# Hybrid block on one core: gate rows through device memory, the last mean square on VectorE, queries turned in the values' bank

## The chip, the core and the metric

One Trainium2 chip, of which one core is used. A core has TensorE (matrix products, written PE in the profile, with its weight loads as PEld), VectorE (DVE), ScalarE (ACT), GpSimd (POOL) and SyncE (SP), which issues most transfers, and 16 DMA engines. The engines run side by side, each its own instructions in order, and wait for each other through semaphores. TensorE writes to PSUM, which has eight banks of 512 fp32 columns on 128 partitions; everything else lies in SBUF, and the weights come from device memory. The metric is the time of one execution on the device in microseconds (us), as the median of several runs.

## The reference

One layer on 256 tokens of width 2048, in fp32: a normalised and modulated input is projected by `w_in`, goes through a two-way gated linear recurrence with 16 heads and through windowed attention with 16 query heads over 4 key heads, both results are projected and merged, and the merged sum is projected by `w_out`, scaled by a gate, added to the input and normalised. Cut to the lines that matter for the change:

```python
mod = jax.nn.silu(c) @ w_ada[l] + b_ada[l]
shift, scale, gate = jnp.split(mod[:, None, :], 3, axis=-1)
xn = rmsnorm(h, norm_gain[l]) * (1.0 + scale) + shift
aq, ak, av, ag, hq, hff, hfb, hi, hg, ma, mb = split_columns(xn @ w_in[l])
q = apply_axial_rope(aq.reshape(B, n, ATT_HEADS, ATT_HEAD_DIM), cos, sin) * q_scale
k = apply_axial_rope(ak.reshape(B, n, ATT_KV_HEADS, ATT_HEAD_DIM), cos, sin)
att_branch = window_attention(q, k, v, k_c, v_c, sink_logits[l]) * jax.nn.silu(ag)
...
y_a = hg_branch @ w_o_hgrn_l
y_b = att_branch @ w_o_attn_l
y = jax.nn.sigmoid(m_a + b_m[0]) * y_a + jax.nn.sigmoid(m_b + b_m[1]) * y_b
h = h + gate * (y @ w_out_l)
return rmsnorm(h, final_norm_gain)      # y * rsqrt(mean(y*y) + EPS) * gain
```

## The kernel before

**Weights.** Every fp32 product is made of three products with rounded operands (`mm3`, lines 80 to 83): a high part of each operand and a low rest. `wchunk` (lines 67 to 78) loads a chunk of 512 KB into one of four `raw` buffers, ScalarE rounds it to `wh` (line 74, three buffers) and VectorE takes the rest `wl` (line 75, three buffers). A rounding into a `wh` buffer waits until TensorE has used up the chunk that lay there. Projections accumulate in four PSUM banks (`pj`). The other four banks have one buffer each by tag: `tp` (turnings), `al1` and `al2` (scores and the recurrence's levels), `o` (state products, outputs of the recurrence, values).

**The gate.** `gates` (lines 750 to 758) forms the gate vector on VectorE beside the recurrence, in four pieces of 512 columns. `gate_end` (line 195) turns a piece with four TensorE transposes into the bank `tp` (`tqg`), and VectorE reduces it (`redg`, line 200) into `gcol`, which holds the gate with the channel on the partition, 128 x 16. Just behind the third piece stand the transposes `to` of a recurrence pair (line 696), in the same bank `tp`. Before the output projection the gate is needed as rows that are equal on all partitions: lines 1047 to 1055 make four diagonal matrices from `gcol` on VectorE (`dgm`), multiply each by a matrix of ones on TensorE in plain fp32 (`pg`, 128 x 512, two passes), and ScalarE copies them to `gt`.

**Attention.** A list written by hand sets TensorE's order here (`manual_schedule`, lines 865 to 1011); the scheduler orders ScalarE and VectorE around it, with attention's own work ahead. `alternate(attend(sts), fill(sts), 1)` takes one step of attention, then one weight chunk of filler. `attend` has two steps for each of 32 heads-by-block `n`: the scores (`sc`), and then, for every fourth, the values of the four before (`oba`, 12 products into the bank `o`), followed by the turning of the probabilities of `n - 2` (`tkp`, four transposes into `tp`). `values` ends with VectorE reading `oba` (`br`, line 980), which alone frees the bank `o`. `fill` runs groups 1 to 3 of `group_in`, while attention works on the group before: eight chunks of the query projection, then eight chunks (slots 0 to 7, two halves of four) of the attention gate's projection. Between these chunks the queries of the group are rotated (`rope`, VectorE) and turned: `turn_q(t)` for token blocks 0 and 1 makes four transposes `tkq` (line 914), a rounding on ScalarE (line 916) and the rest on VectorE (line 917, `qTa`). Block 0 is turned after slot 1 and block 1 after slot 3, in the bank `tp`. After the first half of the gate's chunks ScalarE and VectorE finish two heads: a copy and a sum (`hsum`), a sigmoid (`ga`, line 937) and a product (line 938). The sigmoid and the exponential of the scores (line 956) need different function tables on ScalarE, and each change is an ACT_TABLE_LOAD. The rotated queries, `hsum` and `br` share two buffers (tag `bb`).

**The end.** `settle` (line 1059) multiplies the output projection by `gt`, adds the input, and takes the sum of squares with ScalarE (line 1067). For the last 256 columns this is followed by a sum over five partial sums on VectorE (line 1096), a mean on GpSimd (line 178), a power -1/2 on GpSimd (line 179), the scaling and the stores.

Of the kernel before, what the change touches and what calls it, by code (L numbers as in the profile page):

```python
# [7 lines left out]
F32 = mybir.dt.float32  # L8
F32R = mybir.dt.float32r
U8 = mybir.dt.uint8  # L10
AF = mybir.ActivationFunctionType
ALU = mybir.AluOpType
PSUM = bass.MemoryType.PSUM

P = 128
# [22 lines left out]
def block_kernel(ctx: ExitStack, tc: tile.TileContext, x, c, cx, c_ctx, w_ada, b_ada, norm_gain, w_in,  # L38
# [4 lines left out]
    def pl(name, bufs=1, **kw):  # L43
        return tc.tile_pool(name=name, bufs=bufs, **kw)
# [6 lines left out]
    wp = ctx.enter_context(pl("wp"))  # L51
    pj = ctx.enter_context(pl("pj", 4, space=PSUM))
    ps = ctx.enter_context(pl("ps", 1, space=PSUM))

    def row_bcast(src, n):
        return bass.AP(src.tensor, src.offset, [[0, P], [1, n]])
# [136 lines left out]
                dve.scalar_tensor_tensor(acc, wr[:, j, :], cc, acc, op0=ALU.mult, op1=ALU.add)  # L193

    def gate_end(acc, g):
        tq = ps.tile([P, 512], F32, tag="tp", name="tqg")
        for q in range(4):
            pe.transpose(tq[:, q * P: (q + 1) * P], acc[:, q * P: (q + 1) * P], ident)
        red = pad.tile([P, 4], F32, tag="redg", name="redg")
        dve.tensor_reduce(red, tq.rearrange("p (q k) -> p q k", q=4), mybir.AxisListType.X, ALU.add)  # L200
        gv = gcol[:, 4 * g: 4 * g + 4]
        dve.tensor_tensor(gv, red, gv, op=ALU.add)
# [8 lines left out]

    cg = pad.tile([P, KT], F32, name="cg")
    gcol = few.tile([P, KT], F32, name="gcol")

    FIRST = (("F0", 2), ("F1", 1), ("F0", 2))
    with pl("st", reuse_waits="tile") as st:
# [533 lines left out]
    def gates():  # L750

        for g in range(4):
            for k0 in range(0, KT, 2):
                gate_chunk(accT[:, 0, :], g, k0)
                yield
            gate_end(accT[:, 0, :], g)
        while True:
            yield

# [105 lines left out]
    with tc.manual_schedule(engines={mybir.EngineType.PE}):  # L865
# [29 lines left out]
        def keys():  # L895
            for t in range(4):
# [5 lines left out]
                split(dst[0], dst[1], tk.rearrange("p (j t) -> p j t", j=4))  # L902
                yield

        def group_in(j, st):

            bq = yield from proj_tok_g(w_in, C_Q + 512 * j, x_st, range(2))
            def turn_q(t):
                qr = base.tile([P, 4, HD], F32, tag="bb", name="qr", bufs=2)
                rope(qr, bq[t], t)  # L910
                yield
                tk = ps.tile([P, 512], F32, tag="tp", name="tkq")
                for i in range(4):
                    pe.transpose(tk[:, i * P: (i + 1) * P], qr[:, i, :], ident)
                qh, ql = [X[:, t].rearrange("p h t -> p (h t)") for X in st["q"]]
                act.activation(qh, tk, AF.Copy, scale=HD ** -0.5)
                dve.scalar_tensor_tensor(ql, tk, HD ** -0.5, qh.bitcast(F32), op0=ALU.mult, op1=ALU.subtract)

            turning = [turn_q(t) for t in range(2)]
            next(turning[0])  # L920
            st["q"] = [at.tile([P, 2, 4, P], F32R, tag=tg, name="qTa") for tg in Q_TAGS[j % 2]]
            st["g"] = gt_tile(j, [P, 4, T], "ga")
            for hf in range(2):
                bg = proj_col_x_g(w_in, C_G + 512 * j + 256 * hf)
                for k0 in range(0, KT, 4):
                    next(bg)
                    yield
                    if (hf, k0) == (0, 4):
                        next(turning[0], None)
                    if (hf, k0) == (0, 0):  # L930
                        next(turning[1])
                    if (hf, k0) == (0, 12):
                        next(turning[1], None)
                for i, b in enumerate(result(bg)):
                    gs = halves_sum(b, "bb", 2)
                    gi = st["g"][:, 2 * hf + i, :]
                    act.activation(gi, gs, AF.Sigmoid)
                    dve.tensor_tensor(gi, gi, gs, op=ALU.mult)
# [78 lines left out]
    for t in range(2):  # L1017
        nc.sync.dma_start(xv[t], x[t * P: (t + 1) * P, :])
        nc.sync.dma_start(fg[t], row_bcast(fin_gain[t * 1024: (t + 1) * 1024], 1024))

    def part_b(n):
        by = proj_tok(w_oa, n * 512, b_st, range(2))
# [21 lines left out]
        sl = slice(t * P, (t + 1) * P)  # L1044
        return XH[:, kt, sl], XL[:, kt, sl]

    ones = base.tile([P, 512], F32, tag="sm", name="ones", bufs=3)[:, :P]
    pool.memset(ones, 1.0)
    for n in range(4):
        pg = ps.tile([P, 512], F32, tag="o", name="pg")  # L1050
        dg = base.tile([P, 4, P], F32, tag="bb", name="dgm", bufs=2)
        for q in range(4):
            dve.tensor_scalar(dg[:, q, :], ident, gcol[:, 4 * n + q: 4 * n + q + 1], None, op0=ALU.mult)
        pe.matmul(pg, ones, dg.rearrange("p q c -> p (q c)"), start=True, stop=True)
        act.activation(gt[n // 2][:, (n % 2) * 512: (n % 2 + 1) * 512], pg, AF.Copy)
    fin = few.tile([P, 14], F32, name="fin")
    ssf = fin[:, :10].rearrange("p (t n) -> p t n", t=2)
    rsf = fin[:, 10:12]
    def settle(t, bo, c0, width, slot, gain=True):

        cl = slice(c0, c0 + width)
        ch = slice(c0 % 1024, c0 % 1024 + width)
        ht = base.tile([P, 512], F32, tag="bb", name="ht", bufs=2)[:, :width]
        dve.tensor_tensor(ht, bo, gt[c0 // 1024][:, ch], op=ALU.mult)
        dve.tensor_tensor(xv[t][:, cl], xv[t][:, cl], ht, op=ALU.add)
        sq = base.tile([P, 512], F32, tag="sm", name="fsq", bufs=3)[:, :width]
        act.activation(sq, xv[t][:, cl], AF.Square, accum_out=ssf[:, t, slot: slot + 1])
        if gain:
            dve.tensor_tensor(xv[t][:, cl], xv[t][:, cl], fg[c0 // 1024][:, ch], op=ALU.mult)

# [16 lines left out]
            split(bH[:, ks, :], bL[:, ks, :], rv)  # L1087
    for t in range(2):
        settle(t, bo[t][:, :256], D - 512, 256, 3)
    for t in range(2):  # L1090
        be = bank()
        for kt in range(KT):
            mm3(be[:, :256], y_st(kt, t), (bH[:, kt, :], bL[:, kt, :]), kt == 0, kt == KT - 1)
        settle(t, be[:, :256], D - 256, 256, 4, False)
        tot = fin[:, 12 + t: 13 + t]
        dve.tensor_reduce(tot, ssf[:, t, :], mybir.AxisListType.X, ALU.add)
        rs = rsf[:, t: t + 1]
        rstd_of(tot, D, rs)
        for c0, c1, on_act in ((0, 512, True), (512, 1024, False), (1024, 1536, True), (1536, D, False)):
            o_ = xv[t][:, c0: c1]  # L1100
            if on_act:
                act.activation(o_, o_, AF.Copy, scale=rs)
            else:
                e = min(c1, D - 256)
                dve.tensor_scalar(xv[t][:, c0: e], xv[t][:, c0: e], rs, None, op0=ALU.mult)
                if e < c1:
                    dve.scalar_tensor_tensor(xv[t][:, e: c1], xv[t][:, e: c1], rs, fg[1][:, e - 1024: c1 - 1024],
                                             op0=ALU.mult, op1=ALU.mult)
            (nc.scalar if on_act else nc.sync).dma_start(out[t * P: (t + 1) * P, c0: c1], o_)
# [53 lines left out]
```

## Time and profile before

| | |
|---|---|
| median of 3 runs | 1657.49 us (1657.47 to 1657.75) |
| the profiled execution, whole | 1657.43 us |
| its span in the trace | 1655.7 us |
| TensorE busy | 1632.2 us of the span (99%) |
| VectorE, ScalarE, GpSimd busy | 969.2 us, 750.8 us, 34.5 us |
| DMA | 274.16 MB, mean 166 GB/s |

The span is what the trace covers; 1.7 us of the execution lie around it. A row of a timeline gives the start of an instruction (us from the start of the span), its duration, the engine, the line and what it writes and reads; in brackets stands how long the engine sat idle before it and whom it waited for. Matmuls overlap: the next of 512 columns starts 0.23 us after the one before, though each is shown with 0.39 us, so a loss on TensorE is read from the starts. The granted clock (PEclk) is 1.00 at 2.4 GHz and 0.50 at 1.2 GHz.

### The profile page before, as it was taken

How to read it: one execution, taken by the hardware profiler on the slowest of the kernel's cores; microseconds unless marked ns; L12 is line 12 of the kernel's file. 1: busy time of each engine (PE TensorE's matmuls, PEld its weight loads, DVE VectorE, ACT ScalarE, POOL GpSimd, SP SyncE). 2: the span in 40 equal slices, each digit the busy share in tenths (PEclk: the TensorE clock that was granted, in tenths of full speed). 3: DMA queues.
4: the chain of work that ended last, by engine and by line, in shares of the span. 5: the costliest groups of instructions: out<-in, count | busy, mean ns of one | idle time of the engine just before them, and what ended most of it. 6: DMA issues, size and time to landing. Idle time of an engine off the chain costs nothing.

```text
span 1655.7 us, 22835 instructions
## 1 busy us (share of the span) xinstructions
PE 1632.2 (99%) x8897; PEld 1345.2 (81%) x8897; DVE 969.2 (59%) x1511; ACT 750.8 (45%) x1143; POOL 34.5 (2%) x88
## 2 busy tenths in 40 slices
PE   7999999999999999999999999999999999999997
PEld 4558888888888888888888888888888888788887
DVE  4444577636765466754667555325677676555565
ACT  4333444324443344423455443223576787444443
POOL 2000000000000000000000000000000000000000
PEclk9999999999999999999999999999999999999999
DMA  9993444346344453435345666434544455665554
GB/s 357 382 382 113 147 138 148 102 127 191 91 127 127 149 175 98 139 102 168 125 117 159 185 195 196 129 102 137 171 139 152 132 165 156 207 205 190 179 180 138
DMA packets 191100, 274.16 MB, mean 166 GB/s; under 512 B 9728, under 2 KB 112400, under 8 KB 190224
## 3 DMA queue, kind: packets, MB, share of 16 engines
q1 hardware_dynamic: 189344, 269.39, 51.3%
q0 software_dynamic: 928, 2.20, 0.5%
q8 instruction: 70, 1.15, 0.3%
q10 hardware_dynamic: 720, 1.11, 0.2%
q14 instruction: 38, 0.31, 0.1%
HBM read 270.57 MB, written 2.10 MB: 165 GB/s over the span
## 4 chain that ended last, share of the span: by engine, by line
PE 97%; DVE 1%; DMA 1%; ACT 1%; issue 0%; POOLq 0%; POOL 0%; ACTq 0%
PE pj L81 23%; PE pj L82 23%; PE pj L83 23%; PE pj L139 7%; PE pj L144 3%; PE al L556 2%; PE pa L301 2%; PE pj L391 1%; PE tkp L970 1%; PE pj L384 1%; PE sb L633 1%; PE pj L385 1%; DMA raw<-in_w_ada_dram 1%; PE sc L83 0%; PE ob L674 0%; PE sc L81 0%
## 5 line engine op out<-in xcount | busy, mean ns | idle before, releaser
L75 DVE TENSOR_TENSOR wl<-raw,wh 128x1024 fp32r<-128x1024 f32 x392 | 479.1, 1223 | 430.9 <-ACT wh L74 430.6
L74 ACT ACTIVATE wh<-raw 128x1024 fp32r<-128x1024 f32 x392 | 414.7, 1058 | 576.7 <-PE pj L83 415.9
L83 PE MATMUL pj<-wh,xHL 128*128 128x512 f32 (+1 forms) x1024 | 396.8, 388 | 0.0
L82 PE MATMUL pj<-wl,xHL 128*128 128x512 f32 (+1 forms) x1024 | 395.7, 387 | 0.4 <-DVE wl L75 0.4
L81 PE MATMUL pj<-wh,xHL 128*128 128x512 f32 (+1 forms) x1024 | 392.2, 390 | 0.0
L83 PEld LDWEIGHTS pj<-wh,xHL 128*128 128x128 f32 x1024 | 192.4, 188 | 39.7 <-issue 0.7
L82 PEld LDWEIGHTS pj<-wl,xHL 128*128 128x128 f32 x1024 | 192.5, 188 | 38.5 <-DVE wl L75 0.7
L81 PEld LDWEIGHTS pj<-wh,xHL 128*128 128x128 f32 x1024 | 192.2, 188 | 38.8 <-issue 1.0
L139 PE MATMUL pj<-xHL,wh 128*128 128x512 f32 x512 | 180.9, 396 | 0.0
L81 PE MATMUL pj<-xHL,wh 128*128 128x512 f32 x416 | 164.4, 395 | 0.0
L83 PE MATMUL pj<-xHL,wl 128*128 128x512 f32 x416 | 162.2, 390 | 0.0
L82 PE MATMUL pj<-xHL,wh 128*128 128x512 f32 x416 | 162.1, 390 | 0.0
L144 PE MATMUL pj<-xHL,wl 128*128 128x256 f32 x512 | 139.3, 282 | 0.0
L139 PEld LDWEIGHTS pj<-xHL,wh 128*128 128x128 f32 x512 | 95.1, 188 | 19.5
L82 PE MATMUL pj<-wl,bH 128*128 128x512 f32 x256 | 100.0, 390 | 0.0
L83 PE MATMUL pj<-wh,bL 128*128 128x512 f32 x256 | 99.7, 389 | 0.0
L144 PEld LDWEIGHTS pj<-xHL,wl 128*128 128x128 f32 x512 | 96.6, 189 | 2.5
L83 PEld LDWEIGHTS pj<-xHL,wl 128*128 128x128 f32 x416 | 78.1, 188 | 16.4
L81 PEld LDWEIGHTS pj<-xHL,wh 128*128 128x128 f32 x416 | 78.2, 188 | 15.7
L82 PEld LDWEIGHTS pj<-xHL,wh 128*128 128x128 f32 x416 | 78.2, 188 | 15.5
L81 PE MATMUL pj<-wh,bH 128*128 128x512 f32 x256 | 89.9, 390 | 0.1
L599 DVE TENSOR_TENSOR A<-A,X 128x512 f32<-128x512 f32 x96 | 62.0, 687 | 15.9 <-ACT so L533 6.1
(272 smaller groups left out, 1749.7 us busy)
## 6 DMA issues: line engine op xcount, KB each, us to landing
raw<-in_w_in_dram SPq DMA_DIRECT2D x292, 512.0 KB, 3.6
raw<-in_w_ada_dram SPq DMA_DIRECT2D x128, 256.0 KB, 5.4
raw<-in_w_ada_dram SPq DMA_DIRECT2D x32, 512.0 KB, 3.8
raw<-in_w_o_hgrn_dram SPq DMA_DIRECT2D x32, 512.0 KB, 3.7
raw<-in_w_o_attn_dram SPq DMA_DIRECT2D x32, 512.0 KB, 3.8
raw<-in_w_out_dram SPq DMA_DIRECT2D x32, 512.0 KB, 4.4
raw<-in_w_in_dram SPq DMA_DIRECT2D x24, 256.0 KB, 5.5
X<-in_x_dram SPq DMA_DIRECT2D x2, 1024.0 KB, 6.3
```

The source lines that it names most:

```text
L74: act.activation(h[:, :n], raw[:, :n], AF.Copy)
L75: dve.tensor_tensor(lo[:, :n], raw[:, :n], h[:, :n].bitcast(F32), op=ALU.subtract)
L81: pe.matmul(o, s[0], m[0], start=first, stop=False)
L82: pe.matmul(o, s[0], m[1], start=False, stop=False)
L83: pe.matmul(o, s[1], m[0], start=False, stop=last)
L139: pe.matmul(banks[i].rearrange("p (a t) -> p a t", a=2), h[:, j, cs_], xHL[:, :, kt, :T], start=kt == 0, stop=kt == KT - 1)
L144: pe.matmul(banks[i][:, :T], lo[:, j, cs_], xH[:, kt, :T], start=False, stop=False)
L301: pe.matmul(pa[32 * g: 32 * g + 32, : 2 * w], cT[:, k0 + g, :], rv_[:, :, g % nk, :], start=k0 == 0, stop=k0 == KT - 4, tile_position=(0, ...
L384: pe.matmul(o, hw, xH[:, kt, :], start=kt == 0, stop=False)
L385: pe.matmul(o, lo[:, kt - k, cs_], xH[:, kt, :], start=False, stop=False)
L556: pe.matmul(o, ky, mv, start=True, stop=True, tile_position=(0, 64 * c))
L599: dve.tensor_tensor(av, av, f.unsqueeze(3).to_broadcast([P, 2, n2, b]), op=ALU.mult)
```

## The change

Five edits. `gate_end` puts its third piece into the bank `o`. When the gate is complete, GpSimd's queue writes `gcol` to device memory as 16 rows (`gate_rows`), and after attention it reads them back into `gt`, broadcast to all partitions; the diagonal matrices, the products with ones and the copies go. `turn_q` writes into the bank `o`, and a table `TURNS` says for each group after which slots its two blocks are turned. The sum of squares of the last 256 columns is taken by VectorE, the first four partial sums are added and scaled ahead of it, and the mean's last step is one VectorE instruction.

```diff
+    dram = ctx.enter_context(pl("dram", space=bass.MemoryType.DRAM))
...
     def gate_end(acc, g):
-        tq = ps.tile([P, 512], F32, tag="tp", name="tqg")
+        tq = ps.tile([P, 512], F32, tag="o" if g == 2 else "tp", name="tqg")
...
+    gate_rows = dram.tile([KT, P], F32, name="gate_rows")
...
             gate_end(accT[:, 0, :], g)
+        nc.gpsimd.dma_start(gate_rows.rearrange("k p -> p k"), gcol)
         while True:
...
+        TURNS = ((1, 3), (1, 4), (0, 3), (2, 4))
...
-                tk = ps.tile([P, 512], F32, tag="tp", name="tkq")
+                tk = ps.tile([P, 512], F32, tag="o", name="tkq")
...
-                    if (hf, k0) == (0, 4):
-                        next(turning[0], None)
                     if (hf, k0) == (0, 0):
                         next(turning[1])
-                    if (hf, k0) == (0, 12):
-                        next(turning[1], None)
+                    for t in range(2):
+                        if 4 * hf + k0 // 4 == TURNS[j][t]:
+                            next(turning[t], None)
...
         nc.sync.dma_start(fg[t], row_bcast(fin_gain[t * 1024: (t + 1) * 1024], 1024))
+        nc.gpsimd.dma_start(gt[t], row_bcast(gate_rows[8 * t: 8 * t + 8, :], 1024))
...
-    ones = base.tile([P, 512], F32, tag="sm", name="ones", bufs=3)[:, :P]
-    pool.memset(ones, 1.0)
-    for n in range(4):
-        pg = ps.tile([P, 512], F32, tag="o", name="pg")
-        dg = base.tile([P, 4, P], F32, tag="bb", name="dgm", bufs=2)
-        for q in range(4):
-            dve.tensor_scalar(dg[:, q, :], ident, gcol[:, 4 * n + q: 4 * n + q + 1], None, op0=ALU.mult)
-        pe.matmul(pg, ones, dg.rearrange("p q c -> p (q c)"), start=True, stop=True)
-        act.activation(gt[n // 2][:, (n % 2) * 512: (n % 2 + 1) * 512], pg, AF.Copy)
-    fin = few.tile([P, 14], F32, name="fin")
+    fin = few.tile([P, 16], F32, name="fin")
...
-        act.activation(sq, xv[t][:, cl], AF.Square, accum_out=ssf[:, t, slot: slot + 1])
+        if gain:
+            act.activation(sq, xv[t][:, cl], AF.Square, accum_out=ssf[:, t, slot: slot + 1])
+        else:
+            dve.scalar_tensor_tensor(sq, xv[t][:, cl], 1.0, xv[t][:, cl], op0=ALU.mult, op1=ALU.mult,
+                                     accum_out=ssf[:, t, slot: slot + 1])
...
         settle(t, bo[t][:, :256], D - 512, 256, 3)
+        tot = fin[:, 12 + t: 13 + t]
+        dve.tensor_reduce(tot, ssf[:, t, 0:4], mybir.AxisListType.X, ALU.add)
+        dve.tensor_scalar(tot, tot, 1.0 / D, EPS, op0=ALU.mult, op1=ALU.add)
...
         settle(t, be[:, :256], D - 256, 256, 4, False)
-        tot = fin[:, 12 + t: 13 + t]
-        dve.tensor_reduce(tot, ssf[:, t, :], mybir.AxisListType.X, ALU.add)
         rs = rsf[:, t: t + 1]
-        rstd_of(tot, D, rs)
+        dve.tensor_scalar(rs, ssf[:, t, 4:5], 1.0 / D, fin[:, 12 + t: 13 + t], op0=ALU.mult, op1=ALU.add)
+        pool.tensor_tensor(rs, rs, mhalf[:, :1], op=ALU.pow)
```

In the orders below the new kernel's line numbers are 1 to 9 higher than those of the kernel before (L82 to L84 are its three products of `mm3`, L923 its `tkq`, L978 its `tkp`, L988 its `br`).

TensorE, group 1, from the last values products on, before: the turning of block 1 (`tkq`) had come 28 products earlier, after slot 3.

```order
L81 MATMUL oba<-pT,xHL 128x512
L82 MATMUL oba<-pT,xHL 128x512
L83 MATMUL oba<-pT,xHL 128x512
L970 MATMUL tkp<-cs,pr 128x128 x4
L144 MATMUL pj<-xHL,wl 128x256
L139 MATMUL pj<-xHL,wh 128x512
```

The same place now; group 3 reads alike.

```order
L82 MATMUL oba<-pT,xHL 128x512
L83 MATMUL oba<-pT,xHL 128x512
L84 MATMUL oba<-pT,xHL 128x512
L978 MATMUL tkp<-cs,pr 128x128 x4
L923 MATMUL tkq<-cs,qr 128x128 x4
L145 MATMUL pj<-xHL,wl 128x256
L140 MATMUL pj<-xHL,wh 128x512
```

The second turning of these two groups now stands one chunk later, behind the values and the probabilities, in the bank that the values have just filled.

ScalarE at that place in group 1, before, from the first sigmoid of the half to the rounding of `br`:

```order
L937 ACTIVATE ga<-hsum 128x256
L916 ACTIVATE qTa<-tkq 128x512
L153 ACTIVATE hsum<-pj 128x256
L956 ACT_TABLE_LOAD
L956 ACTIVATE pr,mx<-sc,mx 128x512
L957 ACTIVATE mx<-sk,mx 128x1
L74 ACTIVATE wh<-raw 128x1024
L937 ACT_TABLE_LOAD
L937 ACTIVATE ga<-hsum 128x256
L960 ACTIVATE pr<-pr,mx 128x512
L852 ACTIVATE pT<-tkp 128x4x128
L852 ACTIVATE bH<-br 128x4x128
```

And now:

```order
L945 ACTIVATE ga<-hsum 128x256
L75 ACTIVATE wh<-raw 128x1024
L154 ACTIVATE hsum<-pj 128x256
L964 ACT_TABLE_LOAD
L964 ACTIVATE pr,mx<-sc,mx 128x512
L965 ACTIVATE mx<-sk,mx 128x1
L945 ACT_TABLE_LOAD
L945 ACTIVATE ga<-hsum 128x256
L857 ACTIVATE pT<-tkp 128x4x128
L968 ACTIVATE pr<-pr,mx 128x512
L857 ACTIVATE bH<-br 128x4x128
L925 ACTIVATE qTa<-tkq 128x512
```

The queries' rounding moved from between the two sigmoids to the end, and the weight rounding `wh` took its place, ahead of the second `hsum`.

VectorE at that place, before, from the first product with the sigmoid to `br`:

```order
L938 TENSOR_TENSOR ga<-ga,hsum 128x256
L954 TENSOR_SCALAR mx<-mx,sk 128x1
L917 SCALAR_TENSOR_TENSOR qTa<-tkq,qTa 128x512
L154 TENSOR_TENSOR hsum<-pj,hsum 128x256
L958 TENSOR_TENSOR mx<-mx 128x1
L959 RECIPROCAL mx<-mx 128x1
L75 TENSOR_TENSOR wl<-raw,wh 128x1024
L938 TENSOR_TENSOR ga<-ga,hsum 128x256
L980 TENSOR_TENSOR br<-oba,ga 128x512
L853 TENSOR_TENSOR pT<-tkp,pT 128x4x128
```

And now:

```order
L946 TENSOR_TENSOR ga<-ga,hsum 128x256
L962 TENSOR_SCALAR mx<-mx,sk 128x1
L76 TENSOR_TENSOR wl<-raw,wh 128x1024
L155 TENSOR_TENSOR hsum<-pj,hsum 128x256
L966 TENSOR_TENSOR mx<-mx 128x1
L967 RECIPROCAL mx<-mx 128x1
L946 TENSOR_TENSOR ga<-ga,hsum 128x256
L858 TENSOR_TENSOR pT<-tkp,pT 128x4x128
L988 TENSOR_TENSOR br<-oba,ga 128x512
L858 TENSOR_TENSOR bL<-br,bH 128x4x128
L926 SCALAR_TENSOR_TENSOR qTa<-tkq,qTa 128x512
```

`br` stands behind the second product with the sigmoid in both, and now behind `pT` as well.

## Rows read from the trace of the kernel before

**Rows 1.** The page's part 4: the chain that ended last, by engine.
```profile
PE 97%; DVE 1%; DMA 1%; ACT 1%; issue 0%; POOLq 0%; POOL 0%; ACTq 0%
```

**Rows 2.** Waits of TensorE: who for whom, us in total, times, longest.
```profile
PE tkp L970 <- DVE qTa L917: 1.7, 3, 0.6
...
PE to L696 <- DVE redg L200: 0.8, 1, 0.8
...
PE pa L301 <- DMA raw<-in_w_ada_dram: 0.3, 1, 0.3
```

**Rows 3.** Timeline of TensorE, group 1: start, duration, engine, operation, idle before.
```profile
1215.69 0.39 PE L139 MATMUL pj<-xHL,wh 128*128 128x512 f32 x1
1216.65 0.63 PE L970 MATMUL tkp<-cs,pr 128*128 128x128 f32 x4 [0.57 <-DVE qTa L917]
```

**Rows 4.** Timeline of TensorE at one of the four gate products.
```profile
1558.65 1.02 PE L1054 MATMUL pg<-dgm,ones 128*128 128x512 f32 x2
...
1559.74 0.40 PE L81 MATMUL pj<-wh,xHL 128*128 128x512 f32 x1
```

**Rows 5.** Timeline of TensorE at the gate's third piece.
```profile
663.61 0.60 PE L198 MATMUL tqg<-cs,acc 128*128 128x128 f32 x4
665.00 0.65 PE L696 MATMUL to<-cs,so 128*128 128x128 f32 x4 [0.78 <-DVE redg L200]
```

**Rows 6.** Timeline of VectorE at the end, last block of tokens.
```profile
1647.60 0.42 DVE L1065 TENSOR_TENSOR xv<-xv,ht 128x256 f32<-128x256 f32 x1
```

**Rows 7.** The same of GpSimd's power, and a VectorE product of that width.
```profile
1649.12 0.56 POOL L179 TENSOR_TENSOR fin<-fin,mhalf 128x1 f32<-128x1 f32 x1
...
1650.37 0.48 DVE L1107 SCALAR_TENSOR_TENSOR xv<-xv,fin,fg 128x256 f32<-128x256 f32 x1
```

**Rows 8.** Timeline of TensorE, group 1: first values product, first product behind `tkp`.
```profile
1223.83 0.39 PE L81 MATMUL oba<-pT,xHL 128*128 128x512 f32 x1
...
1226.92 0.36 PE L144 MATMUL pj<-xHL,wl 128*128 128x256 f32 x1
```

**Rows 9.** Timeline of ScalarE, group 1, around the two sigmoids.
```profile
1220.10 1.06 ACT L74 ACTIVATE wh<-raw 128x1024 fp32r<-128x1024 f32 x1 [0.50 <-PE pj L139]
...
1223.27 0.38 ACT L153 ACTIVATE hsum<-pj 128x256 f32<-128x256 f32 x1
...
1225.82 1.05 ACT L74 ACTIVATE wh<-raw 128x1024 fp32r<-128x1024 f32 x1
1226.89 1.28 ACT L937 ACT_TABLE_LOAD   x1
1228.18 0.42 ACT L937 ACTIVATE ga<-hsum 128x256 f32<-128x256 f32 x1
...
1229.12 0.58 ACT L852 ACTIVATE pT<-tkp 128x512 fp32r<-128x512 f32 x1
```

**Rows 10.** Timeline of VectorE, group 1: the queries' rest, `br` and `pT`.
```profile
1215.83 0.68 DVE L917 SCALAR_TENSOR_TENSOR qTa<-tkq,qTa 128x512 fp32r<-128x512 f32 x1
...
1228.98 0.68 DVE L980 TENSOR_TENSOR br<-oba,ga 128x512 f32<-128x512 f32 x1
1229.73 0.69 DVE L853 TENSOR_TENSOR pT<-tkp,pT 128x512 fp32r<-128x512 f32 x1
```

**Rows 11.** Timelines of VectorE and TensorE, group 2: queries' rest, first values product.
```profile
1283.81 0.69 DVE L917 SCALAR_TENSOR_TENSOR qTa<-tkq,qTa 128x512 fp32r<-128x512 f32 x1
...
1284.24 0.39 PE L81 MATMUL oba<-pT,xHL 128*128 128x512 f32 x1
```

**Rows 12.** Stretches: PE, PEld, DVE, ACT, POOL busy, granted clock, DMA share, GB/s.
```profile
20.50:21.00 0.50, 0.41 (x2) 0.41 (x3) 0.21 (x2) 0.00 (x0) 0.00 (x0) 0.54 1.10 389
...
23.00:24.00 1.00, 1.00 (x8) 0.00 (x0) 0.00 (x0) 0.00 (x0) 0.00 (x0) 0.52 1.09 384
...
1652.00:1653.00 1.00, 0.00 (x0) 0.00 (x0) 0.00 (x0) 0.00 (x0) 0.00 (x0) 0.55 1.06 330
```

**Rows 13.** Timeline of TensorE ahead of the first of these stretches.
```profile
20.59 1.97 PE L405 MATMUL idle<-cs 128*128 128x128 f32 x8 [2.43 <-DVE cols L252]
```

## The prediction

> **What bounds the kernel now.** I read the chain that ended last first: 97% of it is TensorE [rows 1]. So a saving on another engine is worth nothing by itself, and what counts is what TensorE executes and where it stands still. Then TensorE's own waits: three times `tkp` waits for VectorE's `qTa`, once `to` waits for `redg`, and weights cost it 0.3 us in the whole run [rows 2]. The reader is to see two things there: the change aims at these four waits, and TensorE has almost no other, so that any new wait adds to the time in full. Last I read the timelines of the places that the change moves, on TensorE, ScalarE and VectorE.
>
> **What goes.** Each gate product costs the distance between the starts around it less the one ordinary product that lies between: 1559.74 - 1558.65 - 0.23 = 0.86 us [rows 4]. Four are 3.4 us. VectorE's diagonal matrices and ScalarE's copies go too, worth nothing, since neither engine sets the pace there.
>
> Each wait of `tkp` costs 1216.65 - 1215.69 - 0.23 = 0.73 us [rows 3]; the profile's idle of 0.57 us is less because it counts from the modelled end of the last product. Three are 2.2 us. They go, since `tkq` no longer uses the bank `tp`.
>
> The third piece of the gate: from `tqg` to `to` 1.39 us pass [rows 5], of which four transposes need 0.36 us. (Twelve values products and four transposes take 1226.92 - 1223.83 = 3.09 us [rows 8], less 12 x 0.227 = 2.73 us.) So 1.0 us goes. The bank `o` is next wanted by the state products of that pair, 24 projection products later, when `redg` is long done.
>
> The end: the square would start on VectorE 0.04 us after 1648.02, when the sum before it ends [rows 6], and take up to 0.48 us, as a three-operand product of that width does [rows 7]. A one-column instruction of some 0.2 us and a hop of 0.1 us follow, so the power starts at about 1648.87 instead of 1649.12 [rows 7]. That is 0.25 us; bounds 0 and 0.45 us.
>
> Together 3.4 + 2.2 + 1.0 + 0.25 = 6.9 us.
>
> **What comes: the values' bank.** In groups 1 and 3 the second `tkq` now stands right behind `tkp`, in the bank that the twelve values products have just filled, and may start only when `br` has been read out of it. In the trace before, TensorE was through with `tkp` at 1226.92 [rows 8], while `br` started at 1228.98 and ended at 1229.66 [rows 10]. Nobody on TensorE waited for that; now `tkq` does, and behind it stands the whole stream of projections. `br` is late because VectorE comes to it behind the second product with the sigmoid, and that sigmoid is late because between the two sigmoids ScalarE changes to the exponential's table and back.
>
> The price has a lower bound from the unchanged times: 1229.66, 0.14 us of hop (as from the end of `qTa` at 1216.51 to `tkp` at 1216.65 [rows 3, 10]), less 1226.92, is 2.9 us. The other bound comes from the new order. ScalarE's `wh` now stands ahead of the second `hsum`, and a `wh` waits for TensorE's chunk (as at 1220.10 [rows 9]), here for the one that ends where the values products begin. From that moment on ScalarE and VectorE need: 0.2 us until `wh` starts, 1.0 us for it, then what passed before from `hsum` to the next instruction behind the exponential, 1225.82 - 1223.27 = 2.55 us, 0.1 us until the table load, 1.29 us for it, 0.4 us for the sigmoid, 0.6 us for `pT`'s rounding, 0.65 us for `pT`'s rest on VectorE, now ahead of `br`, 0.65 us for `br`, 0.14 us of hop [rows 9, 10]. That is 7.6 us, while TensorE is ready 3.1 us after that moment [rows 8]: a wait of 4.5 us. I take 4.3 us, near the upper bound, since that one follows the new order and overlaps make it a little shorter. Two such waits are 8.6 us. The trace before has the same pattern in each group, so group 3 costs what group 1 costs.
>
> For one of these steps the Trainium skill has a larger price: its page "ScalarE: Activation LUTs", section "What ACT_TABLE_LOAD costs", gives a load of about 1.28 us and a drain of about 1.38 us for each change of table. The row shows 1.29 us from the start of the load to the start of the sigmoid [rows 9] and no room for the drain; by the page two changes would make each wait 2.8 us longer and the sum 5.5 us higher, and I go by the row.
>
> Group 2 keeps its second turning after slot 3, but now the values products wait for that turning's rest on VectorE. Before, `qTa` ended at 1284.50 and the first values product started at 1284.24 [rows 11]. With TensorE 0.73 us earlier and VectorE unchanged this is a wait of 1284.50 + 0.14 - 1283.51 = 1.1 us; with both earlier by the same it is 0.4 us. The order puts a scaling of the probabilities (0.6 us) ahead of the queries' rounding, so I take 0.9 us. The first turning of group 2 stands a slot earlier and may meet an unfinished rotation: 0.1 us.
>
> **What comes: the gate's rows.** GpSimd issues the write behind the recurrence's work, with nothing urgent behind it but two loads of merge biases, needed some 70 us later. The two reads are 512 KB each like the two of the final gain, and stand ahead of three bias loads. They are needed at the first `settle`, a hundred microseconds later. Cover for all of it is the chunks loaded ahead, which leave TensorE with 0.3 us of waiting for loads in all [rows 2]. I take 0; 0 to 2 us as bounds, the upper for a weight chunk that comes late.
>
> **The sum.** 1657.43 - 6.9 + 8.6 + 0.9 + 0.1 = 1660.1 us, against the profiled execution's own time (its span of 1655.7 us and 1.7 us around it), which stands 0.06 us below the median.
>
> **The clock.** TensorE has no wait as long as these in the middle of the run. At the start it sat idle for 2.43 us until 20.59 [rows 13], and the granted clock fell to 0.50, that is 1.2 GHz, at about 20.5 and rose at about 23.96, by the means of 0.54 and 0.52 in the stretches around [rows 12]. Behind its last product at 1647 it kept 1.00 for almost 5 us and fell at 1652.1 [rows 12]. So an idle time of 4.3 us lies between one that brought a fall and one that did not yet, and may go either way at each of the two places. One spell of 3.4 us at half the clock loses 1.7 us of work, less what of it lies inside the wait. I expect the two waits to cost about one full spell together, 1.7 us; bounds 0 and 3.4 us. The Trainium skill says the same of the direction: "TensorE: Matmul & The Clock Gate", section "HAM oscillation — how this bites in real kernels", has the array return to its slow level after an idle gap and pay the warm-up again behind each. The trace agrees at 20.5 us.
>
> **Forecast and rivals.** Forecast: both waits and the clock's fall behind them, 1660.1 + 1.7 = 1661.8 us, 1660.9 to 1663.5. Chance 0.50.
>
> Rival 1, not slower: the clock stays at 2.4 GHz through both waits. For it speaks the end of the run, against it the start. 1660.1 us, 0.16% over before, within 0.2%, which is about what a measurement of this kernel can tell from no change. Chance 0.22.
>
> Rival 2: the waits are as short as their lower bound because ScalarE and VectorE come through earlier than the new order suggests: 6.9 us less, 5.8 us and 0.5 us more, 1656.8 us, or 1658 us with a short fall of the clock. Against it speaks that the weight rounding ahead of the second `hsum` is tied to TensorE. Chance 0.12.
>
> Rival 3, faster: `br` is read out before TensorE has done `tkp`, so the turnings are free, as the four waits that go would suggest. It would need `br` almost 3 us earlier than in the trace. 1657.43 - 6.9 + 0.5 = 1651.0 us. Chance 0.08.
>
> Rival 4: each wait brings more than a whole spell of half clock, 2 to 3 us of work each: 1664 to 1666 us. It decides if the clock stays at 0.50 for over 3.4 us behind a wait. Chance 0.08.
>
> Leaving out rivals 3 and 4 (0.16), the range is 1657.0 to 1663.8 us. Faster by over 0.2% (under 1654.2): 0.08. Within: 0.22 + 0.12 = 0.34. Slower (over 1660.8): 0.50 + 0.08 = 0.58.
>
> **What would show it.** In the trace of the changed kernel: TensorE's waits should list `tkq` for `br` twice with about 4.3 us each, and `oba` for `qTa` once under 1 us; `tkp` for `qTa` and `to` for `redg` should be gone; between two products of the output projection no 0.86 us should be left; and in the stretches behind the two waits the granted clock should be 0.50 for some microseconds. I am wrong if `tkq` starts within 1 us of `tkp`'s end, if its wait has another releaser, or if weights or `gt` show up among TensorE's waits.

## The result and the profile after

The changed kernel takes **1663.37 us** (1662.96 to 1663.98), the kernel before 1657.61 us in the same series: ratio 1.0035 [1.0022, 1.0048] (in brackets the 95% interval), 5.8 us slower. The profiled execution of the changed kernel took 1663.35 us with a span of 1661.6 us. The forecast was 1661.8 us with a range of 1657.0 to 1663.8 us.

TensorE's waits come first, as in [rows 2]: who for whom, us in total, times, longest.

```profile
PE tkq L923 <- DVE br L988: 8.3, 2, 4.1
...
PE oba L82 <- DVE qTa L926: 0.8, 1, 0.8
PE pa L304 <- DMA raw<-in_w_ada_dram: 0.7, 2, 0.4
```

The waits that the change aims at (`tkp` for `qTa`, `to` for `redg`) are gone. In their place stands one line that was not there: `tkq` waits for `br` twice, each time for longer than all four old waits together (1.7 + 0.8 us [rows 2]). `oba` for `qTa` is the other new one.

Timeline of TensorE in group 1, the first values product, both turnings and the next scores (start, duration, engine, line, in brackets the idle time before):

```profile
1221.74 0.39 PE L82 MATMUL oba<-pT,xHL 128*128 128x512 f32 x1
...
1224.49 0.60 PE L978 MATMUL tkp<-cs,pr 128*128 128x128 f32 x4
1229.22 0.94 PE L923 MATMUL tkq<-cs,qr 128*128 128x128 f32 x4 [4.13 <-DVE br L988]
...
1234.05 0.39 PE L82 MATMUL sc<-xHL,qTa 128*128 128x512 f32 x1
```

`tkp` needs 0.36 us, so the loss is 1229.22 - 1224.49 - 0.36 = 4.37 us, in group 3 the same (`tkp` 1350.85, `tkq` 1355.58).

What `br` waits for stands on ScalarE and then VectorE, group 1:

```profile
1221.94 1.06 ACT L75 ACTIVATE wh<-raw 128x1024 fp32r<-128x1024 f32 x1 [0.70 <-PE pj L140]
1222.90 0.36 ACT L154 ACTIVATE hsum<-pj 128x256 f32<-128x256 f32 x1
1223.28 1.28 ACT L964 ACT_TABLE_LOAD   x1
1224.58 0.69 ACT L964 ACTIVATE pr<-sc,mx 128x512 f32<-128x512 f32 x1
...
1225.56 1.28 ACT L945 ACT_TABLE_LOAD   x1
1226.85 0.42 ACT L945 ACTIVATE ga<-hsum 128x256 f32<-128x256 f32 x1
1227.17 0.58 ACT L857 ACTIVATE pT<-tkp 128x512 fp32r<-128x512 f32 x1
```

```profile
1227.30 0.43 DVE L946 TENSOR_TENSOR ga<-ga,hsum 128x256 f32<-128x256 f32 x1 [1.37 <-ACT ga L945]
1227.78 0.69 DVE L858 TENSOR_TENSOR pT<-tkp,pT 128x512 fp32r<-128x512 f32 x1
1228.39 0.68 DVE L988 TENSOR_TENSOR br<-oba,ga 128x512 f32<-128x512 f32 x1
```

The reader sees one unbroken chain, from the weight rounding that TensorE releases at 1221.94 through two table loads, the sigmoid and the rounding of `pT` on ScalarE to the rest of `pT` and `br` on VectorE, which ends at 1229.07. This is the chain that the prediction added up: from the first values product to `tkq` it takes 1229.22 - 1221.74 = 7.48 us, against its 7.6.

The granted clock behind the wait, by stretches with the columns of [rows 12]:

```profile
1224.00:1229.00 5.00, 1.09 (x7) 0.69 (x5) 2.56 (x7) 4.32 (x8) 0.00 (x0) 1.00 0.41 125
1229.00:1230.00 1.00, 0.78 (x5) 0.81 (x6) 0.30 (x2) 0.63 (x1) 0.00 (x0) 0.70 0.00 0
1230.00:1231.00 1.00, 1.00 (x5) 0.90 (x5) 0.64 (x2) 0.60 (x1) 0.00 (x0) 0.50 0.00 0
...
1232.00:1233.00 1.00, 1.00 (x5) 0.86 (x4) 0.00 (x0) 0.00 (x0) 0.00 (x0) 0.59 0.00 0
1233.00:1234.00 1.00, 1.00 (x7) 0.90 (x6) 0.00 (x0) 0.00 (x0) 0.00 (x0) 1.00 0.00 0
```

Through the whole wait the clock is 1.00. A mean of 0.70 from 1229 to 1230 means that it fell to 0.50 at about 1229.40, when TensorE was at work again, and 0.59 from 1232 to 1233 that it rose at about 1232.8. From `tkq` to the next scores now 1234.05 - 1229.22 = 4.83 us pass. The same instructions at full clock take 3.25 us (an experiment below), so the spell costs 1.58 us. Group 3 has the same spell and the same 4.83 us.

Group 2, VectorE and TensorE, as in [rows 11]:

```profile
1287.97 0.69 DVE L926 SCALAR_TENSOR_TENSOR qTa<-tkq,qTa 128x512 fp32r<-128x512 f32 x1 [0.67 <-ACT qTa L925]
```

```profile
1287.56 0.40 PE L140 MATMUL pj<-xHL,wh 128*128 128x512 f32 x1
1288.72 0.50 PE L82 MATMUL oba<-pT,xHL 128*128 128x512 f32 x1 [0.76 <-DVE qTa L926]
```

The loss is 1288.72 - 1287.56 - 0.23 = 0.93 us.

What was gained: TensorE at the gate's third piece, as in [rows 5], then the gate rows' transfers, and the end, as in [rows 6, 7].

```profile
663.71 0.60 PE L200 MATMUL tqg<-cs,acc 128*128 128x128 f32 x4
664.15 0.60 PE L699 MATMUL to<-cs,so 128*128 128x128 f32 x4
```

```profile
gt<-gate_rows POOLq DMA_DIRECT2D x2, 512.0 KB, 4.8
gate_rows<-gcol POOLq DMA_DIRECT2D x1, 8.0 KB
```

```profile
1653.82 0.42 DVE L1065 TENSOR_TENSOR xv<-xv,ht 128x256 f32<-128x256 f32 x1
...
1655.04 0.56 POOL L1105 TENSOR_TENSOR fin<-fin,mhalf 128x1 f32<-128x1 f32 x1 [5.18 <-DVE fin L1104]
```

From `tqg` to `to` there are 0.44 us instead of 1.39, and from the last sum on VectorE to the power 1655.04 - 1653.82 = 1.22 us instead of 1649.12 - 1647.60 = 1.52 [rows 6, 7]. The reads of the gate rows take 4.8 us each, and nobody waits for them.

### The profile page after: what moved, and what is told of

Same layout as the page of the kernel before. It is cut to its first block, busy times and chain, and to the rows that moved or that the text cites. A ratio compares the mean times of both kernels' runs of the same rounds, so it can differ in the third digit from the quotient of the medians.

```text
span 1661.6 us, 22807 instructions
## 1 busy us (share of the span) xinstructions
PE 1631.7 (98%) x8889; PEld 1346.9 (81%) x8889; DVE 968.2 (58%) x1503; ACT 744.7 (45%) x1133; POOL 34.8 (2%) x88
## 3 DMA queue, kind: packets, MB, share of 16 engines
q0 software_dynamic: 1264, 3.25, 1.0%
q8 instruction: 70, 1.15, 0.3%
## 4 chain that ended last, share of the span: by engine, by line
PE 94%; DMA 3%; ACT 1%; DVE 1%; issue 1%; POOLq 0%; POOL 0%; SPq 0%; ACTq 0%
PE pj L82 23%; PE pj L84 23%; PE pj L83 23%; PE pj L140 7%; PE pj L145 4%; DMA raw<-in_w_ada_dram 3%; PE al L559 2%; PE pa L304 1%; PE pj L394 1%; PE sb L636 1%; PE tkp L978 1%; PE pj L387 1%; PE pj L388 1%; DMA X<-in_x_dram 0%; PE ob L677 0%
## 5 line engine op out<-in xcount | busy, mean ns | idle before, releaser
L84 PE MATMUL pj<-wh,xHL 128*128 128x512 f32 (+1 forms) x1024 | 395.4, 386 | 0.0
L82 PE MATMUL pj<-wh,xHL 128*128 128x512 f32 (+1 forms) x1024 | 391.0, 390 | 0.0
L84 PEld LDWEIGHTS pj<-wh,xHL 128*128 128x128 f32 x1024 | 192.4, 188 | 39.1
L82 PEld LDWEIGHTS pj<-wh,xHL 128*128 128x128 f32 x1024 | 192.2, 188 | 38.0 <-DVE yt L1034 0.4
L82 PE MATMUL pj<-xHL,wh 128*128 128x512 f32 x416 | 164.3, 395 | 0.0
L84 PE MATMUL pj<-xHL,wl 128*128 128x512 f32 x416 | 162.1, 390 | 0.0
L84 PE MATMUL pj<-wh,bL 128*128 128x512 f32 x256 | 99.7, 389 | 0.0
L84 PEld LDWEIGHTS pj<-xHL,wl 128*128 128x128 f32 x416 | 78.1, 188 | 16.4
L82 PEld LDWEIGHTS pj<-xHL,wh 128*128 128x128 f32 x416 | 78.2, 188 | 15.6
L82 PE MATMUL pj<-wh,bH 128*128 128x512 f32 x256 | 89.9, 390 | 0.1
```

The lines of the kernel that those rows point to most:

```text
L82: pe.matmul(o, s[0], m[0], start=first, stop=False)
L84: pe.matmul(o, s[1], m[0], start=False, stop=last)
```

## Experiments

### Each part alone

Four kernels add one part of the change to the kernel before. The gate rows through device memory alone (the diagonal matrices, products and copies go):

```diff
+        nc.gpsimd.dma_start(gate_rows.rearrange("k p -> p k"), gcol)
...
+        nc.gpsimd.dma_start(gt[t], row_bcast(gate_rows[8 * t: 8 * t + 8, :], 1024))
```

> The kernel before with the gate's rows through device memory alone. Theory A: four products of 0.86 us go, nothing comes: 1654.2 us, 1653.9 to 1654.6. Theory B (the write of 2048 single values and the two broadcast reads delay weight chunks or bias rows): 1655 us or more, and a wait of TensorE for weights in the trace.

Measured: 1654.34 us (1653.97 to 1655.51), ratio 0.998 [0.997, 0.999], 3.2 us less than before. The four gate products were worth 3.4 us, and the transfers cost nothing that can be measured.

The bank of the gate's third piece alone:

```diff
-        tq = ps.tile([P, 512], F32, tag="tp", name="tqg")
+        tq = ps.tile([P, 512], F32, tag="o" if g == 2 else "tp", name="tqg")
```

> The kernel before with the gate's third piece turned in the bank o alone. The wait of to for redg goes, 1.0 us on TensorE: 1656.6 us, 1656.3 to 1656.9. If VectorE's work behind it takes the place of the wait: 1657.4 us or more.

Measured: 1656.59 us (1656.23 to 1658.37), ratio 0.9994 [0.9984, 1.0003]: 1.0 us less by the medians, as expected, though the interval reaches across no change.

The end alone (the last square and mean on VectorE):

```diff
+            dve.scalar_tensor_tensor(sq, xv[t][:, cl], 1.0, xv[t][:, cl], op0=ALU.mult, op1=ALU.mult,
+                                     accum_out=ssf[:, t, slot: slot + 1])
```

> The kernel before with the last sum of squares on VectorE alone. The trace of the changed kernel has 1.81 us from the last sum to the scaling where before it was 2.11 us: 1657.3 us, 1657.0 to 1657.5. If the earlier steps on VectorE held up the last block's product: no change.

Measured: 1657.37 us (1657.02 to 1658.27), ratio 0.9998 [0.9989, 1.0008]. The time can't tell 0.3 us from nothing; that gain rests on the trace's rows above.

The turnings alone, bank and places:

```diff
+        TURNS = ((1, 3), (1, 4), (0, 3), (2, 4))
...
-                tk = ps.tile([P, 512], F32, tag="tp", name="tkq")
+                tk = ps.tile([P, 512], F32, tag="o", name="tkq")
```

> The kernel before with the turning edit alone (the values' bank and the table of places). Theory A: everything that the change loses is in this edit, and it loses more than the whole change, since the other edits gain 3.4 + 1.0 + 0.3 us: 1668.1 us, 1667.5 to 1668.8. Theory B: under 1660 us.

Measured: 1668.74 us (1667.96 to 1669.32), ratio 1.0066 [1.0049, 1.0083], 11.0 us more than before. Its trace shows the same waits as the whole change, and two spells at 0.50 as well:

```profile
PE tkq L916 <- DVE br L981: 8.3, 2, 4.1
...
PE oba L81 <- DVE qTa L919: 0.8, 1, 0.8
```

So one part makes the loss; of the three others the gate rows clearly gain, and the bank and the end gain too little for their times to tell. Together the parts give -3.2 - 1.0 - 0.2 + 11.0 = +6.6 us, the whole change +5.8 us; the 0.8 us between lie within the spread of the fourth kernel's own runs (1.4 us).

### Is it the bank or the places?

First the changed kernel with the places of the kernel before, still in the values' bank:

```diff
-        TURNS = ((1, 3), (1, 4), (0, 3), (2, 4))
+        TURNS = ((1, 3), (1, 3), (1, 3), (1, 3))
```

> The changed kernel with every group's queries turned after slots 1 and 3, as before the change, but still in the values' bank; all other edits kept. Theory A (the loss is tkq waiting for br in groups 1 and 3, 4.4 us on TensorE each, and 1.6 us of half clock behind each): both waits and both spells go; the values products may wait up to 0.9 us for the queries' rest in each of three groups, 0.3 us likely. 1651.5 us, 1651.0 to 1653.2. Theory B (the loss lies in the gate's rows through device memory or in the values' bank as such): it stays, over 1656 us.

Measured: 1651.86 us (1651.61 to 1651.95), ratio 0.9964 [0.9951, 0.9977]. The wait for `br` is gone; in the list of TensorE's waits this is left of the new ones:

```profile
PE oba L82 <- DVE qTa L926: 0.5, 3, 0.2
```

Then with both turnings a slot earlier still in the last three groups:

```diff
+        TURNS = ((1, 3), (0, 2), (0, 2), (0, 2))
```

> The changed kernel with groups 1 to 3 turned after slots 0 and 2, that is behind the two turnings of probabilities that lie between two values. Theory A: no wait of the values for the queries' rest or the other way round, at most 0.2 us per group for an unfinished rotation: 1651.2 us, 1650.7 to 1652.0, within 0.5 us of the run with slots 1 and 3. Theory B: over 1656 us.

Measured: 1650.71 us (1650.59 to 1650.93), ratio 0.9958 [0.9943, 0.9973]. In the stretch from 1200 to 1400 us, which holds the attention of these groups, TensorE is now busy all the time, where in the changed kernel it idles for 9 us and has a mean clock of 0.98. The first row is this kernel's, the second the changed kernel's (columns of [rows 12]).

```profile
1200.00:1400.00 200.00, 200.00 (x1035) 169.12 (x1034) 148.39 (x286) 143.47 (x241) 0.60 (x1) 1.00 0.48 150
```

```profile
1200.00:1400.00 200.00, 190.98 (x976) 161.21 (x976) 139.41 (x268) 139.27 (x231) 0.60 (x1) 0.98 0.46 140
```

It is the fastest of all the kernels here: 7.0 us under the kernel before, 12.7 us under the change, for one line of numbers. It is also 1.15 us under the kernel with slots 1 and 3, where at most 0.5 us was expected; the three waits of `oba` there, 0.32 us each by the starts, account for most of it.

The places of the change with the turnings back in the bank `tp`:

```diff
-                tk = ps.tile([P, 512], F32, tag="o", name="tkq")
+                tk = ps.tile([P, 512], F32, tag="tp", name="tkq")
```

> The changed kernel with tkq put back into the bank tp, everything else as changed, the new places too. It tells the bank from the places. Theory A (the places are at fault: at them any one bank is still waiting to be read): behind tkp the bank tp is free only when VectorE has taken pT's rest, at about 1228.5 in group 1 of the changed kernel, against 1229.2 for br; so tkq waits some 3.6 us there, 2 to 3 us at other places where it follows a tkp, and tkp waits again behind a tkq. By a replay of the instructions with the durations of the trace: 3.6 + 3.2 + 2.8 + 2.2 + 0.6 = 12.4 us of waits in place of 8.3 + 0.8 us, so 1663.4 + 3.3 = 1666.7 us, and up to 5 us more or 3 us less by where the clock falls: 1664 to 1672 us. Theory B (the values' bank is at fault, the places are harmless): the waits of tkq go and three waits of tkp of 0.6 us return, so 1663.4 - 8.7 - 0.8 - 3.2 + 2.2 = 1652.9 us.

Measured: 1667.89 us (1667.39 to 1669.71), ratio 1.0063 [1.0048, 1.0078]; the profiled execution was the longest of them. TensorE's waits in it:

```profile
PE tkq L923 <- DVE pT L858: 10.9, 4, 3.4
...
PE tkp L978 <- DVE qTa L926: 0.6, 1, 0.6
```

In the old bank the new places wait for another reader (`pT` instead of `br`), four times, and longer in sum. So the bank as such is not at fault. What decides is whether a turning stands close behind the transposes or products that filled its bank, while the bank's reader is still queued on a busy engine.

One slot later in groups 1 and 3, with the values' bank:

```diff
+        TURNS = ((1, 3), (1, 5), (0, 3), (2, 5))
```

> The changed kernel with the second turning of groups 1 and 3 one chunk later, after slot 5 instead of 4; the bank and everything else kept. Theory A: a chunk of 2.9 us now lies between the probabilities and the queries' transposes, so that the wait for br shrinks from 4.1 us to 0.7 to 1.4 us and the clock does not fall: 1663.4 - 2 x (2.9 + 1.6) = 1654.4 us, 1653.0 to 1655.0. If the clock falls even after short waits: 1657 us or more. If the bank costs the same wherever it stands: 1663 us.

Measured: 1653.33 us (1653.09 to 1653.56), ratio 0.9974 [0.9963, 0.9984], 10 us under the change. One more chunk of products now lies ahead of the turning. TensorE's wait for `br`:

```profile
PE tkq L923 <- DVE br L988: 1.3, 2, 0.7
```

The wait is 0.65 us at either place, and both spells at half the clock are gone (mean 1.00 from 1200 to 1400 us). `br` isn't earlier: from the end of `tkp` to `tkq` there are still 4.37 us (group 3: `tkp` 1346.01, `tkq` 1350.74), but 3.57 us of them are now filled by a chunk and the next scores. So the wait shrinks by just the work put ahead of it, and the clock's fall goes with it as a whole: 2 x 3.57 + 2 x 1.58 = 10.3 us, measured 10.0.

### Is the clock's fall a cost of its own?

The changed kernel with the values products ahead of both long waits made twice. The second set starts the sum anew and writes the same values again and is useless work (24 products); nothing else in the program differs.

```diff
-                for kt in range(4):
-                    mm3(ob, v_st(kt, j), [X[:, kt].rearrange("p h t -> p (h t)") for X in pT], kt == 0, kt == 3)
+                for _ in range(2 if m in (0, 4) else 1):
+                    for kt in range(4):
+                        mm3(ob, v_st(kt, j), [X[:, kt].rearrange("p h t -> p (h t)") for X in pT], kt == 0, kt == 3)
```

> The changed kernel with the twelve values products ahead of the two waits made twice (24 useless products, 5.4 us of TensorE's work). Theory A with the clock: each wait shrinks by the 2.7 us that now fill it, to 0.8 to 1.7 us, and the clock has no reason to fall, so that 2 x 1.6 us come back: 1658.8 to 1660.3 us, faster than the changed kernel though it does more. Theory A without the clock (the spells cost nothing): 1663.4 us, 0.5 us either way. If the products came on top of the waits: 1668.8 us.

Measured: 1659.11 us (1658.88 to 1659.77), ratio 1.0009 [0.9999, 1.0018] to before and 4.3 us under the change, with more to do. Its timelines of TensorE and VectorE in group 1, and the clock behind the wait:

```profile
1222.03 0.39 PE L82 MATMUL oba<-pT,xHL 128*128 128x512 f32 x1
...
1227.50 0.60 PE L978 MATMUL tkp<-cs,pr 128*128 128x128 f32 x4
1228.87 0.66 PE L923 MATMUL tkq<-cs,qr 128*128 128x128 f32 x4 [0.77 <-DVE br L989]
```

```profile
1228.13 0.69 DVE L989 TENSOR_TENSOR br<-oba,ga 128x512 f32<-128x512 f32 x1
1228.77 0.69 DVE L858 TENSOR_TENSOR pT<-tkp,pT 128x512 fp32r<-128x512 f32 x1
```

```profile
1229.00:1230.00 1.00, 1.00 (x8) 0.96 (x9) 0.95 (x2) 0.91 (x2) 0.00 (x0) 1.00 0.00 0
```

Useless products (2.73 us) and the wait left behind them (1228.87 - 1227.50 - 0.36 = 1.01 us) take 3.74 us at each place, against 4.37 us of waiting. That is 1.3 us less for two, and not the products' doing: the scheduler's order came out different, with `br` ahead of `pT` on VectorE, and the chain from the first values product to `tkq` is shorter by one such instruction (1228.87 - 1222.03 = 6.84 us instead of 7.48). The products themselves only fill time in which TensorE would have waited. The other 3.0 us of the 4.3 are the two spells at half the clock, which the changed kernel's rows put at 3.2 us.

### What makes `br` late?

The changed kernel with a copy instead of the attention gate's sigmoid, which leaves the sigmoid out of the computation. The order on every engine stays, only the table loads go.

```diff
-                    act.activation(gi, gs, AF.Sigmoid)
+                    act.activation(gi, gs, AF.Copy)
```

> The changed kernel with the attention gate's sigmoid replaced by a plain copy, so that ScalarE needs no change of function table between the exponentials; this leaves the sigmoid out of the computation. The order on every engine stays, but for the table loads. It asks how much of each wait of tkq for br is the two table loads. In the trace of the changed kernel br starts at 1228.39 behind this chain: wh until 1222.98, hsum, table load 1.28, exponential, table load 1.28, sigmoid, product, pT, br. Without the loads VectorE's sum of 1224.17 to 1224.59 sets when the copy can start, then copy, product, pT and br take 0.42, 0.43, 0.65 and 0.65 us, and br ends at about 1226.85 and tkq starts at about 1227.0 instead of 1229.22. Theory A (the loads stand on the path that frees the bank): each loss at tkq falls from 4.37 to about 2.1 us, that is 4.4 us for both. If the clock no longer falls (idle about 1.9 us), another 3.2 us go: 1655.8 us, range 1654.5 to 1656.8; if it still falls at both places 1659.0 us. Theory B (br is late for another reason, the loads are hidden): the waits stay at 4.1 us and the time at 1663.4 us within 0.7.

Measured: 1657.52 us, ratio 0.9999 [0.9990, 1.0009] to before. Its ten runs spread from 1655.99 to 1659.65, wider than those of the other kernels but of the same order as the two spells. Timeline of TensorE, the turnings in group 1 and in group 3:

```profile
1225.19 0.60 PE L978 MATMUL tkp<-cs,pr 128*128 128x128 f32 x4
1227.89 0.63 PE L923 MATMUL tkq<-cs,qr 128*128 128x128 f32 x4 [2.10 <-DVE br L988]
...
1231.14 0.39 PE L82 MATMUL sc<-xHL,qTa 128*128 128x512 f32 x1
```

```profile
1347.16 0.60 PE L978 MATMUL tkp<-cs,pr 128*128 128x128 f32 x4
1349.86 1.09 PE L923 MATMUL tkq<-cs,qr 128*128 128x128 f32 x4 [2.10 <-DVE br L988]
```

The loss falls from 4.37 to 1227.89 - 1225.19 - 0.36 = 2.34 us, so the two loads (1.28 us each) hold 2.0 us of each wait. What is left is the rest of the chain. Theory A holds, and theory B falls. The stretches behind the two waits:

```profile
1228.00:1229.00 1.00, 1.00 (x8) 0.95 (x9) 0.55 (x1) 0.85 (x2) 0.00 (x0) 1.00 0.01 4
```

```profile
1350.00:1351.00 1.00, 1.00 (x6) 1.00 (x7) 0.59 (x1) 0.40 (x2) 0.00 (x0) 0.50 0.08 20
```

Two waits of the same 2.10 us in one execution: behind the first the clock held, behind the second it fell. Group 1 gives the undisturbed 1231.14 - 1227.89 = 3.25 us used above. The expectation had 1655.8 us without a fall and 1659.0 us with two; this execution, with one, took 1657.64 us. That the runs spread from 1655.99 to 1659.65 because some had no fall and some two fits these prices, but only one of them has a trace. The mean granted clock of the others points the same way: the three runs over 1658.5 us have 0.994 to 0.995, the seven others 0.996 to 0.998.

## Why the prediction was right

**The mechanism** was right. Each mark that the prediction named is in the trace: `tkq` for `br` twice with over 4 us, `oba` for `qTa` once under 1 us, both old waits gone, no gate product left, half the clock behind both waits. The places experiments show it from the other side: without the waits for `br` the change takes 1651.86 us, close to the 1651.0 us of rival 3, which saw the turnings as free. That rival had the right price for another set of places.

**The savings.** Taken 6.9 us. The gate rows alone gave 3.2 us for the 3.4 of the four products, the bank 1.0 for 1.0, and the end's rows 0.30 for 0.25 (the steps that the prediction names add up to 1648.84 and 0.28 us, not 1648.87). The three waits of `tkp` (2.2 us) are gone from the list.

**The wait for `br`.** Taken 4.3 us between 2.9 and 4.5, measured 4.37 us twice. The choice of the upper bound carried the forecast. The lower one assumed that `br` keeps its time, while the new order puts `wh` behind TensorE and everything else behind `wh`; the trace shows just that chain, and the kernel with `br` ahead of `pT` has a chain 0.64 us shorter, as the prediction's 0.65 us for `pT`'s rest would have it. So rival 2 (the lower bound) fell; its 1656.8 us stood 0.2 us outside the range, which was meant to leave out rivals 3 and 4 alone. On the table loads the Trainium skill's page "ScalarE: Activation LUTs", section "What ACT_TABLE_LOAD costs", has a drain of about 1.38 us beside each load. No run shows it: the exponential starts 1224.58 - 1223.28 = 1.30 us after its load, and two loads less shortened a wait by 2.0 us.

**Group 2.** Taken 0.9 us, measured 0.93. For the first turning 0.1 us was taken, and no such wait is in the list.

**The gate's rows.** Taken 0 (0 to 2), and the part alone shows 0 within 0.2 us. The 0.7 us that TensorE waits for `w_ada`'s weights, 0.3 before, don't come from them: the kernels with the bank alone and the end alone wait 0.7 us there too. The prediction's "almost no other" wait and "0.3 us of waiting for loads in all" leave out the start of the program, where TensorE waits 6.1 us for constants and 2.4 us for `cols` in the trace before; the change doesn't touch these.

**The clock** is the term that was mis-sized: 1.7 us taken for both places, 2 x 1.58 = 3.2 us measured. Two things in that step were off. It let the fall happen at either place with an even chance; it came at both. And it counted on a part of a spell that lies inside the wait; here there is none, since the fall came just behind the wait (at 1229.40, when TensorE had begun again at 1229.22). That part isn't always nothing. With the turnings alone the clock fell at about 1230.56 in group 1, 0.65 us before TensorE began again, and rose at about 1233.98, so that only 2.8 us of the spell lie on work:

```profile
1231.21 1.09 PE L916 MATMUL tkq<-cs,qr 128*128 128x128 f32 x4 [4.14 <-DVE br L981]
```

```profile
1230.00:1231.00 1.00, 0.00 (x0) 0.00 (x0) 1.00 (x2) 0.35 (x1) 0.00 (x0) 0.78 0.00 0
```

Its two spells cost 1.28 and 1.39 us (4.53 and 4.64 us from `tkq` to the next scores). The prediction's bounds of 0 to 3.4 us held, and only because they were that wide did the range hold, with 0.4 us to spare. Rival 1 (the clock holds, 1660.1 us) fell, and so did rival 4, since no spell lasted much over 3.4 us.

**The sum** with the measured waits and spells, and the savings as taken, is 1657.43 - 6.9 + 2 x 4.37 + 0.93 + 3.16 = 1663.4 us, against 1663.35 us for the profiled execution. Of the 1.6 us between forecast and result 1.5 are the clock's.

## What to carry to other kernels

When an instruction moves to another PSUM bank, ask who reads that bank last and what is queued ahead of that reader, and add up that queue from the moment that releases it, not from the old times. TensorE, which sets the pace here, paid for each long wait twice: 4.37 us of standing still, and 1.58 us of slower clock around its end. So one slot later was worth 10 us and the slots 1 and 3 were worth 11.5, and it pays to try the neighbouring places before judging the idea.

## What the runs showed of the hardware

**The clock fell around the end of a wait, not at its start.** At the waits of 4.13 and 4.14 us it fell 0.2 and 0.1 us after TensorE had begun again in the changed kernel, and 0.65 and 0.4 us before that with the turnings alone; at the one of 2.10 us with a fall (no sigmoid, 0.92 as the mean of 1349 to 1350) just as it began. In the kernel with the turnings in `tp` it fell behind all four waits, of 3.44, 2.87, 2.57 and 2.03 us; behind the last two 1.3 us later, in the middle of dense work (the last wait ended at 1362.01; stretches of that kernel):

```profile
1362.00:1363.00 1.00, 0.99 (x8) 0.94 (x9) 0.69 (x1) 0.87 (x2) 0.00 (x0) 1.00 0.11 41
1363.00:1364.00 1.00, 1.00 (x7) 0.86 (x6) 0.66 (x1) 0.30 (x1) 0.00 (x0) 0.65 0.06 16
1364.00:1366.00 2.00, 2.00 (x8) 1.71 (x8) 0.03 (x1) 0.00 (x0) 0.00 (x0) 0.50 0.00 0
1366.00:1367.00 1.00, 1.00 (x5) 0.86 (x5) 0.00 (x0) 0.00 (x0) 0.00 (x0) 0.65 0.00 0
```

Means of 0.65 at both ends put 0.50 from about 1363.3 to 1366.7, 3.4 us, as behind the other waits. Of two waits of 2.10 us one brought a fall and one did not, and none of 0.65 to 0.77 us in attention (four places) did. The start of the program has the same mixture: behind an idle time of 2.20 us in the changed kernel (until 20.45) the clock fell at about 21.1, behind one of 2.21 us in the kernel with the bank alone (until 20.73) it stayed at 1.00, and in the kernel with the values made twice it fell at about 15.8, behind idle times of 0.80 and 0.92 us that ended at 13.67 and 15.24. So the length of the last wait alone does not tell whether the clock falls. And a loss of up to 1.6 us can stand a microsecond behind its cause, in a stretch in which TensorE waits for nobody.

**Useless products made a kernel faster.** They cost nothing, since they filled idle time, and the clock stayed at 1.00, which gave back about 3.0 us; the other 1.3 us of the 4.3 come from the changed order on VectorE.
